# Moving the memory's preparation ahead of the second latent keys in a two-layer decoder trunk

## The chip, the cores and the metric

The kernel runs on one core of a Trainium2 chip. The time is that of the device in microseconds, from one launch, as the median of several executions. The engines are TensorE (PE, matrix products; PEld its weight loads), VectorE (DVE), ScalarE (ACT), GpSimd (POOL) and SyncE (SP). [...]

## The reference

Two layers over 512 tokens of width 1024, in float32. A layer has three attention branches that share one input `h = RMSNorm(x)`, and then an MLP:

```python
dq, dk, dv, c_q, c_kv_kr, xq, gate_logits = split(h @ w_in)
y_diff = diff_attention(dq, dk, dv) @ w_diff_o             # 8 heads, two softmax maps each
y_mla  = latent_attention(c_q, c_kv_kr) @ w_mla_o          # 8 heads, keys and values from a 256-wide latent
mem_n  = rmsnorm(mem, mem_gain)                            # 256 fixed memory tokens
y_mem  = memory_cross_attention(xq, mem_n, w_mem_kv) @ w_cross_o   # 4 heads
x = x + (sig(g0)*y_diff + sig(g1)*y_mla + sig(g2)*y_mem) @ w_out
x = x + relu(rmsnorm(x) @ w1)**2 @ w2
```

The memory is the same in both layers; its gain and its weights `w_mem_kv` are the layer's own. Its keys and values depend on nothing that the layer computes from `x`.

## The kernel before

The activations lie transposed, 512 tokens along the free dimension in tiles of 128 x 512. Every float32 operand of a large product is split into a rounded part and a remainder (`split_into`, `split_scaled`: the first on ScalarE, L103 and L107, the second on VectorE, L104 and L108), and each product is three matmuls (`mm3`, L111 to L113). Weights are loaded by SyncE into five tiles `wraw`, and split into `whi` and `wlo`, three tiles deep.

**The order of the work.** The program is a list of entries, each with a function that emits instructions and the weight pieces it takes. The list is written by hand: for each layer come the two latents and their statistics (`ck_item`, `cq_item`, `stats`, `ck_finish`, `cq_finish`), and then the phases of `PLAN` (L25). A phase is a string of groups; `gx:1` takes one entry of the group `gx`. A phase also has a list of attention units, and `merge` (L47) deals the string's entries out evenly among the units. The groups that matter here:

- `gx`: eight gate products of the latent branch (`gate_item`): 24 matmuls of 128 x 512 into one accumulator `psacc`, then VectorE (L783) and a tanh on ScalarE (L784).
- `K0`, `K1`: the keys and values of heads 0 to 3 and 4 to 7 from the latent (`kvb_item`). For each of four token blocks: one accumulator, a copy of the key half into a tile of the pool `O` (L499), a split of the value half into tiles of the pool `B` (L107, L108). Then the keys' squares, their norms, the normed keys in four `O` tiles, and four transposes (`heads_T`, L484) that ScalarE copies into four `B` tiles (L100).
- `Q0`, `Q1`: the queries of the same heads (`qb_item`), in the same manner, with four `O` tiles (L535) and four `B` tiles (L100).
- `mem`: the memory's two preparing entries, held in a list called `pre`, and its eight projection entries (`mem_chunk`).

`pre` holds `mem_stats` (layer 0 alone) and `mem_begin`. `mem_stats` reads the memory in four pieces on ScalarE's DMA queue into `B` tiles (L209), squares each into a further `B` tile with a running sum (L210), and ends with a power on POOL. `mem_begin` transfers the transposed memory in four pieces into `B` tiles (L328), and splits each with the layer's gain in two halves into a pair of `O` tiles (L107, L108); the eight `O` tiles are read by the projection.

Phase 0 has no attention units. Phase 1 has those of heads 0 to 3 of the latent attention (`mla_att`): scores (L624, L627), maximum, exponential (L641), a scaling (L100), and in every second unit transposes of the probabilities (L668), their splits, the product with the values into `pso`, and its split into `O` tiles.

**What decides when an instruction runs.** The entries give every instruction a place in the order; a scheduler with a timing model then deals them out to the engines at compile time and may let a later one go ahead of an earlier one that isn't ready. Every tile belongs to a pool with a fixed number of slots: `O` 16, `B` 40, `scr` 5, `P` 3; in PSUM `psacc` 2, `pss` 3, `pstp` 2 and `pso` 1. A tile gets its slot when it is first filled, and gives it back after its last reader.

Of the kernel before, what the change touches and what calls it, by code (L numbers as in the profile page):

```python
# [21 lines left out]
MEM = 256  # L22
EPS = 1e-6
NEG = -1.0e30
PLAN = ["gx:1 K0 gx:1 Q0 gx:1 K1 gx:1 Q1", "gx mem", "xq h0 v0", "h1 ym", "v1 h2 gc:5", "h3 v2 h4 gc:3", "h5 v3 h6 gc", "h7 gd:5", "gd"]  # L25

C_MIX, C_MLP, C_MEM, C_B, C_QA, C_KVA, C_DO, C_MQ, C_MK, C_CQ, C_CK, C_N = 0, 8, 16, 24, 48, 51, 53, 54, 55, 56, 57, 58

# [18 lines left out]
def merge(att, gemm):  # L47
    if not att:
        return gemm
    out, n, m = [], len(att), len(gemm)  # L50
    j = 0
    for i, a in enumerate(att):
        out.append(a)
        while j < m and j * n < (i + 1) * m:
            out.append(gemm[j])
            j += 1
    out.extend(gemm[j:])
    return out
# [3 lines left out]
def tile_trunk(ctx: ExitStack, tc: tile.TileContext, x_t, mem_t, mem_n, pos, ifr, gcol, grow, w_ck, w_cq, w_kvb, w_qb,  # L62
# [27 lines left out]
    def ct(name, shape, dt=F32):  # L90
        return cst.tile(shape, dt, tag=name, name=name)
# [32 lines left out]
    gc = ct("gc", [P, L, C_N])  # L124
# [79 lines left out]
    def mem_stats():  # L204
        sq4 = small("mss4", 4, 1)
        for t in range(2):
            for j in range(2):
                mt, junk = tl("B"), tl("B")
                A.dma_start(out=mt, in_=mem_n[t * P:(t + 1) * P, j * 512:(j + 1) * 512])  # L209
                A.activation(out=junk, in_=mt, func=AF.Square, accum_out=sq4[:, 2 * t + j:2 * t + j + 1])  # L210
        ss = small("mss", 2, 1)
        V.tensor_reduce(out=ss, in_=sq4.rearrange("p (t j) -> p t j", t=2), axis=AX.X, op=ALU.add)
        ms = small("msm", 2, 1)
        V.tensor_scalar(ms, ss, 1.0 / D, EPS, ALU.mult, ALU.add)
        mst["r"] = small("rmem", 2, 1)
        rsq(mst["r"], ms, 2)
        mst["eps"] = small("epsm", 2, 1)
        V.tensor_scalar(mst["eps"], ms, EPS, None, ALU.mult)
# [64 lines left out]
    def layer(l):  # L283
# [93 lines left out]
        def xq_chunk(c):  # L377
            def done(tp, q):
                if tp == 0:
                    s["xq", c] = [tl("B") for _ in range(2)]  # L380
                y = tl("scr")
                A.activation(out=y, in_=q, func=AF.Copy)
                z = tl("scr")
                A.activation(out=z, in_=y, func=AF.Square)
                ss = small("ss", 8, 4)
                V.tensor_reduce(out=ss[:, :4], in_=z.rearrange("p (g d) -> p g d", d=128), axis=AX.X, op=ALU.add)
                e = small("e", 8, 4)
                V.tensor_tensor(out=e[:, :4].rearrange("p (t h) -> p t h", t=2), in0=ss[:, :4].rearrange("p (t h) -> p t h", t=2),
                                in1=s["ex128"][:, 2 * tp:2 * tp + 2].unsqueeze(2).broadcast_to([P, 2, 2]), op=ALU.add)
                f = small("f", 8, 4)  # L390
                rsq(f[:, :4], e[:, :4], 4)
                yv = y.rearrange("p (g d) -> p g d", d=128)
                V.tensor_tensor(out=yv, in0=yv, in1=f[:, :4].unsqueeze(2).broadcast_to([P, 4, 128]), op=ALU.mult)
                tp_ = ps("tp")
                for h in range(2):
                    for t in range(2):
                        T.transpose(tp_[:, h * 256 + t * P:h * 256 + (t + 1) * P], in_=yv[:, t * 2 + h, :], identity=ident)
                for h in range(2):
                    scale_to(s["xq", c][h][:, tp * 256:(tp + 1) * 256], tp_[:, h * 256:(h + 1) * 256], col(C_CQ))
            return chunk256(w_xq[l, c], x_h, 4, done)  # L400
# [157 lines left out]
        def v_chunk(p):  # L558
            def done(tp, q):
                if tp == 0:  # L560
                    s["dv", p] = [tl("B") for _ in range(2)]
                for ti in range(2):
                    t = 2 * tp + ti
                    A.activation(out=s["dv", p][tp][:, ti * 256:(ti + 1) * 256], in_=q[:, ti * 256:(ti + 1) * 256], func=AF.Copy, scale=s["r"][:, t:t + 1])
            return chunk256(w_d[l, 8 + p], x_h, 4, done)
# [180 lines left out]
        def diff_att(h):  # L746
            p, hh = h // 2, h % 2

            def unit(qi):
                def fn(w):  # L750
                    if qi == 0:
                        s["co"], s["cs"] = ps("o"), small("osum", 8, 3)
                    N = P * (qi + 1)
                    o, cs = s["co"], s["cs"].rearrange("p (m q) -> p m q", m=2)
                    qh, ql, kk = s["dh", h]
                    v_ = s["dv", p]
                    W = max(N, 256)
                    qk = [([z[m][:, qi * P:(qi + 1) * P] for z in (qh, ql)], kk[m][:, :W]) for m in range(2)]
                    vf = lambda j: v_[j // 2][:, (j % 2) * 256 + hh * P:(j % 2) * 256 + (hh + 1) * P]
                    pt = scores(N, qk, True, [cs[:, m, qi:qi + 1] for m in range(2)], True)  # L760
                    pv_tok(pt, qi + 1, o[:, qi * P:(qi + 1) * P], vf)
                    if qi == NT - 1:
                        oc = o_copy()
                        z = tl("scr")
                        A.activation(out=z, in_=oc, func=AF.Square)
                        ss = small("ss", 8, 4)
                        V.tensor_reduce(out=ss[:, :4], in_=z.rearrange("p (g d) -> p g d", g=4), axis=AX.X, op=ALU.add)
                        e = small("e", 8, 4)
                        V.tensor_tensor(out=e[:, :4], in0=cs[:, 0, :], in1=cs[:, 0, :], op=ALU.mult)
                        V.scalar_tensor_tensor(out=e[:, :4], in0=e[:, :4], scalar=128.0 * EPS, in1=ss[:, :4], op0=ALU.mult, op1=ALU.add)  # L770
                        f = small("of", 8, 3)
                        rsq(f[:, :4], e[:, :4], 4)
                        o_finish(oc, f[:, :4], 4, dgain[:, l:l + 1], "od")
                return Entry(fn)
            return [unit(q) for q in range(NT)]

        def gate_item(b, ft, where):
            def fn(w):
                q = ps("acc")
                for k in range(KT):  # L780
                    mm3(q, (w[0][0][:, k, :], w[0][1][:, k, :]), s["h"][k], k == 0, k == KT - 1)
                g = tl(where)
                V.tensor_tensor(out=g, in0=q, in1=s["R"], op=ALU.mult)  # L783
                A.activation(out=g, in_=g, func=AF.Tanh, scale=0.5, bias=hb[:, l, b * 8 + ft:b * 8 + ft + 1])  # L784
                s["g", b, ft] = g
            return Entry(fn, [w_g[l, b * 8 + ft]])
# [10 lines left out]
        def y4_item(w_o, key, b, fp, first):  # L797
            def fn(w):
                for i in range(2):
                    q = ps("acc")  # L800
                    for k in range(4):
                        mm3(q, (w[0][0][:, i * 4 + k, :], w[0][1][:, i * 4 + k, :]), s[key][k], k == 0, k == 3)
                    y_mix(q, b, 2 * fp + i, first)
            return Entry(fn, [w_o[l, fp]])
# [154 lines left out]
        def gy4(w_o, key, b, first):  # L959
            r = []  # L960
            for fp in range(4):
                r += [gate_item(b, 2 * fp, "G"), gate_item(b, 2 * fp + 1, "G"), y4_item(w_o, key, b, fp, first)]
            return r

        e = [Entry(lambda w: begin())]
        gx = [gate_item(1, ft, "X") for ft in range(KT)]
        ym = [y4_item(w_om, "om", 1, fp, True) for fp in range(4)]
        gc_ = gy4(w_oc, "oc", 2, False)
        gd = [gate_item(0, ft, "B") for ft in range(KT)]
        cross = sum([cross_att(h) for h in range(4)], [])  # L970
        mem = sum([mem_chunk(c) for c in range(4)], [])
        e += [Entry(ck_item, [w_ck[l][:, 0:2, :], w_ck[l][:, 2:5, :], w_ck[l][:, 5:8, :]]), cq_item(0), Entry(lambda w: stats()), cq_item(1), Entry(lambda w: ck_finish()), cq_item(2), Entry(lambda w: cq_finish())]
        pre = ([Entry(lambda w: mem_stats())] if l == 0 else []) + [Entry(mem_begin)]
        K0, K1, Q0, Q1 = [kvb_item(0)], [kvb_item(1)], [qb_item(0)], [qb_item(1)]
        xq = xq_chunk(0) + xq_chunk(1)
        groups = {"gx": gx, "K0": K0, "K1": K1, "Q0": Q0, "Q1": Q1, "mem": pre + mem, "xq": xq, "ym": ym, "gc": gc_, "gd": gd}
        groups.update({f"v{p}": v_chunk(p) for p in range(4)}, **{f"h{h}": head_chunk(h) for h in range(8)})

        def take(spec):
            r = []  # L980
            for t in spec.split():
# [6 lines left out]
                  diff_att(4) + diff_att(5), diff_att(6) + diff_att(7), []]  # L988
        for a, sp in zip(phases, PLAN):
            e += merge(a, take(sp))  # L990
# [16 lines left out]
    for l in range(L):  # L1007
        prog.extend(layer(l))
# [157 lines left out]
```

## Time and profile before

| | |
|---|---|
| median of 3 runs | 1997.16 us (1996.64 to 2002.54) |
| the profiled execution: time, span | 1999.83 us, 1998.0 us |
| PE busy | 1956.1 us, 98% of the span |
| DVE, ACT, POOL busy | 68%, 52%, 15% |
| mean granted clock of TensorE | 0.997 |
| DMA | 181.20 MB, mean 91 GB/s |

A row of the order in time has the start in us, the duration, the engine, the line and operation, the tiles as out<-in, their shapes, a count, and in brackets the engine's idle time just before and what ended it. `ACTq` is ScalarE's queue of instructions as it issues a DMA. Names are given without their numbers, so that `B` stands for any tile of the pool `B`. Layer 0 ends at about the middle of the span: what happens at 77 us in layer 0 happens at 1071 us in layer 1.

### The profile page before, as it was taken

To read this page: it belongs to the slowest core of one execution; us is meant where nothing else is said; L and a number is where in the kernel's file an instruction comes from. 1 tells how busy PE (TensorE), PEld (TensorE's weight loads), DVE (VectorE), ACT (ScalarE), POOL (GpSimd) and SP (SyncE) were. 2 spreads that over 40 slices of the span, in tenths; PEclk is the share of its full clock that TensorE was granted. 3 is DMA by queue.
4 is the path that set the end of the run, shared out by engine and by line. 5 is a ranking of instruction groups with operands and counts; after the bars stand their busy time and mean duration, and the time that the engine had idled before them with its cause. 6 is when DMAs were issued, how large, how long until landed. Compare 5 with 4: busy or idle time off the path is not lost.

```text
span 1998.0 us, 30334 instructions
## 1 busy us (share of the span) xinstructions
PE 1956.1 (98%) x11888; PEld 1739.9 (87%) x11888; DVE 1352.1 (68%) x2431; ACT 1029.5 (52%) x1929; POOL 305.6 (15%) x209
## 2 busy tenths in 40 slices
PE   8999999999999999999999999999899999999999
PEld 7779989888888899999888899988888888999997
DVE  7756677687745866666657667677777458666665
ACT  5666765555533533344456667555555335344332
POOL 0300101111100222222002001011111002222220
PEclk9999999999999999999999999999999999999999
DMA  5233122222224233333432321121222332232232
GB/s 182 69 112 106 64 64 72 67 69 70 74 64 158 64 106 106 97 104 95 132 113 68 119 92 55 64 76 63 64 74 79 101 126 75 96 106 96 95 107 83
DMA packets 54687, 181.20 MB, mean 91 GB/s; under 512 B 6417, under 2 KB 7441, under 8 KB 54545
## 3 DMA queue, kind: packets, MB, share of 16 engines
q1 hardware_dynamic: 51840, 175.66, 27.2%
q10 hardware_dynamic: 2704, 3.62, 0.6%
q8 instruction: 93, 1.52, 0.3%
q14 instruction: 50, 0.40, 0.1%
HBM read 175.06 MB, written 4.19 MB: 90 GB/s over the span
## 4 chain that ended last, share of the span: by engine, by line
PE 90%; DVE 5%; ACT 2%; issue 1%; DMA 1%; ACTq 0%; DVEq 0%
PE psacc L111 20%; PE psacc L112 20%; PE psacc L113 20%; PE pss L113 5%; PE pss L111 5%; PE pss L112 5%; PE pss L627 2%; PE pso L656 2%; PE pss L624 1%; PE pstp L113 1%; PE pstp L112 1%; PE pstp L111 1%; PE pstp L668 1%; DVE wlo L104 1%; PE pstp L652 1%
## 5 line engine op out<-in xcount | busy, mean ns | idle before, releaser
L103 ACT ACTIVATE whi<-wraw 128x1024 fp32r<-128x1024 f32 (+1 forms) x362 | 378.7, 1047 | 522.6 <-PE psacc L112 225.0
L104 DVE TENSOR_TENSOR wlo<-wraw,whi 128x1024 fp32r<-128x1024 f32 (+1 forms) x362 | 444.6, 1228 | 126.1 <-ACT whi L103 124.4
L111 PE MATMUL psacc<-B,whi 128*128 128x512 f32 x1072 | 421.2, 393 | 2.7 <-DVE G L783 2.7
L112 PE MATMUL psacc<-B,whi 128*128 128x512 f32 x1072 | 419.5, 391 | 0.0
L113 PE MATMUL psacc<-B,wlo 128*128 128x512 f32 x1072 | 418.6, 390 | 0.0
L111 PE MATMUL psacc<-whi,B 128*128 128x256 f32 (+3 forms) x1008 | 302.0, 300 | 14.7 <-ACT whi L103 6.9
L112 PE MATMUL psacc<-wlo,B 128*128 128x256 f32 (+3 forms) x1008 | 295.5, 293 | 1.2 <-DVE wlo L104 1.2
L113 PE MATMUL psacc<-whi,B 128*128 128x256 f32 (+3 forms) x1008 | 293.4, 292 | 0.0
L1055 POOL TENSOR_TENSOR wraw<-wraw,wraw 128x1024 f32<-128x1024 f32 x56 | 152.7, 2726 | 572.0 <-DVE wlo L104 501.9
L111 PEld LDWEIGHTS psacc<-B,whi 128*128 128x128 f32 x1072 | 201.6, 188 | 42.9 <-DVE G L783 3.5
L113 PEld LDWEIGHTS psacc<-B,wlo 128*128 128x128 f32 x1072 | 201.4, 188 | 42.2
L112 PEld LDWEIGHTS psacc<-B,whi 128*128 128x128 f32 x1072 | 201.6, 188 | 37.8
L111 PEld LDWEIGHTS psacc<-whi,B 128*128 128x128 f32 x1008 | 192.9, 192 | 22.7 <-ACT whi L103 6.9
L112 PEld LDWEIGHTS psacc<-wlo,B 128*128 128x128 f32 x1008 | 193.1, 192 | 5.0 <-DVE wlo L104 1.5
L113 PEld LDWEIGHTS psacc<-whi,B 128*128 128x128 f32 x1008 | 192.6, 192 | 1.7
L947 DVE TENSOR_TENSOR X<-psacc,X 128x512 f32<-128x512 f32 x128 | 88.3, 690 | 135.3 <-PE psacc L113 135.3
L111 PE MATMUL pss<-O,whi 128*128 128x256 f32 (+1 forms) x528 | 170.2, 323 | 1.6 <-ACT whi L103 0.9
L112 PE MATMUL pss<-O,whi 128*128 128x256 f32 (+1 forms) x528 | 170.3, 322 | 0.0
L113 PE MATMUL pss<-O,wlo 128*128 128x256 f32 (+1 forms) x528 | 169.7, 323 | 0.3 <-DVE wlo L104 0.3
L136 POOL TENSOR_TENSOR f<-e,mhalf 128x8 f32<-128x8 f32 (+1 forms) x60 | 89.3, 1488 | 469.2 <-DVE e L583 270.3
L641 ACT ACTIVATE P<-pss,nmx 128x128 f32<-128x128 f32 (+2 forms) x224 | 115.4, 521 | 47.9 <-DVE nmx L638 35.7
L111 PEld LDWEIGHTS pss<-O,whi 128*128 128x128 f32 x528 | 100.4, 190 | 13.2 <-ACT whi L103 3.5
(250 smaller groups left out, 3563.9 us busy)
## 6 DMA issues: line engine op xcount, KB each, us to landing
wraw<-in_w_dram SPq DMA_DIRECT2D x128, 512.0 KB, 3.5
wraw<-in_w_g_dram SPq DMA_DIRECT2D x48, 512.0 KB, 3.5
wraw<-in_w_d_dram SPq DMA_DIRECT2D x48, 512.0 KB, 3.7
wraw<-in_w_mem_dram SPq DMA_DIRECT2D x16, 512.0 KB, 3.7
wraw<-in_w_od_dram SPq DMA_DIRECT2D x16, 512.0 KB, 3.6
wraw<-in_w_out_dram SPq DMA_DIRECT2D x16, 512.0 KB, 3.9
X<-in_x_t_dram SPq DMA_DIRECT2D x16, 256.0 KB, 5.1
wraw<-in_w_xq_dram SPq DMA_DIRECT2D x8, 512.0 KB, 3.7
```

The source lines that it names most:

```text
L103: A.activation(out=hi, in_=src, func=AF.Copy)
L104: V.tensor_tensor(out=lo, in0=src, in1=hi, op=ALU.subtract)
L111: T.matmul(o, lhsT=l[0], rhs=r[0], start=first, stop=False, **kw)
L112: T.matmul(o, lhsT=l[0], rhs=r[1], start=False, stop=False, **kw)
L113: T.matmul(o, lhsT=l[1], rhs=r[0], start=False, stop=last, **kw)
L136: G.tensor_tensor(out=o, in0=e, in1=mhalf[:, :n], op=ALU.pow)
L624: T.matmul(sw[m][:, :max(N, 256)], lhsT=qk[m][0][i], rhs=qk[m][1], start=i == 0, stop=i == 1)
L627: T.matmul(sv[m], lhsT=qk[m][0], rhs=qk[m][1], start=True, stop=True)
L641: A.activation(out=pt[:, m, :N], in_=sv[m], func=AF.Exp, bias=nmx[:, m:m + 1], accum_out=ssum[m])
L656: T.matmul(o, lhsT=w[:, j * P:(j + 1) * P], rhs=vs(j), start=j == 0, stop=j == nb - 1)
L947: V.tensor_tensor(out=xt, in0=q, in1=xt, op=ALU.add)
L1055: G.tensor_tensor(out=d["t"], in0=src[0]["t"], in1=src[1]["t"], op=ALU.subtract)
```

## The change

The two entries of `pre` become a group of their own. `PLAN` takes it in phase 0, behind the first queries and ahead of the third gate product and the second keys; `mem` keeps the eight projection entries in phase 1. Phase 1 then deals 12 entries out among its eight attention units, where it had 14 in layer 0 and 13 in layer 1.

```diff
-PLAN = ["gx:1 K0 gx:1 Q0 gx:1 K1 gx:1 Q1", "gx mem", "xq h0 v0", ...
+PLAN = ["gx:1 K0 gx:1 Q0 pre gx:1 K1 gx:1 Q1", "gx mem", "xq h0 v0", ...
...
         pre = ([Entry(lambda w: mem_stats())] if l == 0 else []) + [Entry(mem_begin)]
...
-        groups = {"gx": gx, "K0": K0, "K1": K1, "Q0": Q0, "Q1": Q1, "mem": pre + mem, "xq": xq, ...
+        groups = {"gx": gx, "K0": K0, "K1": K1, "Q0": Q0, "Q1": Q1, "pre": pre, "mem": mem, "xq": xq, ...
```

More of the change, by code (lines that the diff above doesn't have):

```diff
@@ L24 @@
 NEG = -1.0e30
-PLAN = ["gx:1 K0 gx:1 Q0 gx:1 K1 gx:1 Q1", "gx mem", "xq h0 v0", "h1 ym", "v1 h2 gc:5", "h3 v2 h4 gc:3", "h5 v3 h6 gc", "h7 gd:5", "gd"]
+PLAN = ["gx:1 K0 gx:1 Q0 pre gx:1 K1 gx:1 Q1", "gx mem", "xq h0 v0", "h1 ym", "v1 h2 gc:5", "h3 v2 h4 gc:3", "h5 v3 h6 gc", "h7 gd:5", "gd"]
 C_MIX, C_MLP, C_MEM, C_B, C_QA, C_KVA, C_DO, C_MQ, C_MK, C_CQ, C_CK, C_N = 0, 8, 16, 24, 48, 51, 53, 54, 55, 56, 57, 58
@@ L975, in layer @@
         xq = xq_chunk(0) + xq_chunk(1)
-        groups = {"gx": gx, "K0": K0, "K1": K1, "Q0": Q0, "Q1": Q1, "mem": pre + mem, "xq": xq, "ym": ym, "gc": gc_, "gd": gd}
+        groups = {"gx": gx, "K0": K0, "K1": K1, "Q0": Q0, "Q1": Q1, "pre": pre, "mem": mem, "xq": xq, "ym": ym, "gc": gc_, "gd": gd}
         groups.update({f"v{p}": v_chunk(p) for p in range(4)}, **{f"h{h}": head_chunk(h) for h in range(8)})
```

## The prediction

> **What bounds the kernel now.** I read the page first, then the busy time by windows around the two places that the change touches, then ScalarE's instructions in order of time, and last TensorE's beside them. From the page:
>
> ```profile
> span 1998.0 us, 30334 instructions
> PE 1956.1 (98%) x11888; PEld 1739.9 (87%) x11888; DVE 1352.1 (68%) x2431; ACT 1029.5 (52%) x1929; POOL 305.6 (15%) x209
> PE 90%; DVE 5%; ACT 2%; issue 1%; DMA 1%; ACTq 0%; DVEq 0%
> ```
>
> TensorE sets the time: 98% busy, 90% of the chain that ended last. No matrix work is added or taken away, so the change can only move TensorE's idle time (42 us in all) and its clock. The windows (columns: stretch, length, busy time by engine, granted clock, DMA share, GB/s) show what the memory's preparation costs where it stands now, first in layer 0, then in layer 1:
>
> ```profile
> 128.30:138.30 10.00, 5.39 (x22) 3.25 (x22) 6.61 (x18) 9.38 (x26) 0.70 (x1) 0.95 0.56 176
> 138.30:143.80 5.50, 5.48 (x25) 5.48 (x26) 4.72 (x11) 5.42 (x15) 0.00 (x0) 0.50 0.17 63
> 1120.00:1128.60 8.60, 7.12 (x34) 4.42 (x32) 6.23 (x14) 7.57 (x20) 0.00 (x0) 1.00 0.42 150
> ```
>
> In layer 0 TensorE idles 10.00 - 5.39 = 4.6 us, while ScalarE is busy 9.38 of 10; behind it follow 5.5 us at a granted clock of 0.50, which is 5.5 x 0.5 = 2.75 us lost. In layer 1, without the statistics, it idles 8.60 - 7.12 = 1.5 us and the clock holds. So 4.6 + 2.75 + 1.5 = 8.9 us is all that a perfect move could win, 0.45% of the time.
>
> Why it is so long in layer 0 is read on ScalarE (L209 reads the memory for its statistics, L210 squares it, L328 transfers the transposed memory, L107 splits it):
>
> ```profile
> 122.36 0.35 ACTq L209 DMA_DIRECT2D B<-in_mem_n_dram  x1
> 122.61 0.71 ACT L784 ACTIVATE X<-X,hb 128x512 f32<-128x512 f32 x1
> 123.22 0.67 ACT L100 ACTIVATE B<-pstp,gc 96x512 f32<-96x512 f32 x1
> 125.04 0.63 ACT L210 ACTIVATE B<-B 128x512 f32<-128x512 f32 x1 [1.14 <-DMA B<-in_mem_n_dram]
> 125.04 0.35 ACTq L209 DMA_DIRECT2D B<-in_mem_n_dram  x1
> ...
> 128.65 0.63 ACT L210 ACTIVATE B<-B 128x512 f32<-128x512 f32 x1 [2.89 <-DMA B<-in_mem_n_dram]
> 128.66 0.33 ACTq L209 DMA_DIRECT2D B<-in_mem_n_dram  x1
> ...
> 131.21 0.34 ACTq L209 DMA_DIRECT2D B<-in_mem_n_dram  x1
> ...
> 134.21 0.65 ACT L210 ACTIVATE B<-B 128x512 f32<-128x512 f32 x1
> 134.42 0.33 ACTq L328 DMA_DIRECT2D B<-in_mem_t_dram  x1
> ...
> 137.76 0.91 ACT L107 ACTIVATE O<-B,gc 128x256 fp32r<-128x256 f32 x2 [0.27 <-DMA B<-in_mem_t_dram]
> ...
> 142.22 0.90 ACT L107 ACTIVATE O<-B,gc 128x256 fp32r<-128x256 f32 x2
> DMA to landing us min/median/max: 2.5/2.6/3.6
> DMA to landing us min/median/max: 3.0/3.8/6.7
> ```
>
> (The last two rows are the landings of the reads for the statistics and of the transfers.) The four reads go out one by one, each together with the square of the one before. The chain from the first read to the first transfer takes 134.42 - 122.36 = 12.1 us, and from there to the end of the last split 143.12 - 134.42 = 8.7 us.
>
> **How tiles are granted.** The reads could have gone out at any time since the start: they depend on nothing. They go out right behind the last copy of a query into a tile of the pool B (L100), and the read that fills a B tile follows the square that fills the B tile named before it. I read this so: the tiles of one pool are granted strictly in the order in which the program names them, each when the first instruction that fills it is placed. The second keys show the same (L499 copies the keys into O, L107 splits the values into B, L100 copies the turned queries into B):
>
> ```profile
> 51.79 0.37 ACT L499 ACTIVATE O<-psacc 128x256 f32<-128x256 f32 x1
> 52.05 0.47 ACT L107 ACTIVATE B<-psacc,skv 128x256 fp32r<-128x256 f32 x1
> ...
> 77.55 0.39 ACT L499 ACTIVATE O<-psacc 128x256 f32<-128x256 f32 x1
> ...
> 82.59 0.68 ACT L100 ACTIVATE B<-pstp,gc 96x512 f32<-96x512 f32 x1 [0.81 <-PE pstp L484]
> 83.17 0.82 ACT L107 ACTIVATE B<-psacc,skv 128x256 fp32r<-128x256 f32 x2
> ...
> 1071.02 0.39 ACT L499 ACTIVATE O<-psacc 128x256 f32<-128x256 f32 x1 [0.36 <-PE psacc L113]
> ...
> 1076.05 0.68 ACT L100 ACTIVATE B<-pstp,gc 96x512 f32<-96x512 f32 x1 [0.81 <-PE pstp L484]
> 1076.64 0.82 ACT L107 ACTIVATE B<-psacc,skv 128x256 fp32r<-128x256 f32 x2
> ```
>
> In the first keys the split follows its copy by 0.3 us. In the second keys it comes 5.6 us after it, in both layers, right behind the fourth query copy, though the product is ready and B has six of its 40 tiles free (16 for the normed input, 4 and 6 for the two latents, 4 values and 4 keys are 34). Only the order explains that. TensorE pays at once, since both accumulators then hold unread keys:
>
> ```profile
> 84.45 0.50 PE L111 MATMUL psacc<-whi,B 128*128 128x512 f32 x1 [1.24 <-DVE B L108]
> 85.94 0.81 PE L627 MATMUL pss<-B,B 96*128 96x384 f32 x2
> 87.97 1.88 PE L627 MATMUL pss<-B,B 96*128 96x512 f32 x4
> 1077.91 0.50 PE L111 MATMUL psacc<-whi,B 128*128 128x512 f32 x1 [1.24 <-DVE B L108]
> ```
>
> **The change part by part.** The instructions are the same; what moves is the place in the order, and with it the place in three queues: ScalarE's, the grant of B and the grant of O.
>
> *What it takes away.* The gaps at 128 to 138 and 1120 to 1128 lose their cause: ScalarE has 4 squares and 8 splits less there. I leave 0.4 and 0.5 us for the attention's own waits: 4.2 and 1.0 us won. The slow clock after the first gap goes too, 2.75 us.
>
> *What it puts behind the second keys, layer 0.* Their values come after the memory's 4 x 2 tiles for the statistics and 4 raw tiles in B, and their key copies after the memory's 8 split tiles in O. So nothing reads the two accumulators until the whole preparation is placed, its last split included. It starts where the fourth query copy is, 82.6. B then has 38 tiles taken, so one read and its square fit at a time. By the measured chain it takes 12.1 us. With the quickest landing and nothing else in the way it takes 4 x 2.5 = 10; with the slowest landing, each read also waiting for the square before it (0.63), 4 x 4.2 = 17. I take 12.5, near the measured chain. The transfers and splits took 8.7 us between the attention's work; by themselves they take the first landing, 137.76 - 134.42 = 3.3, and 8 x 0.45 = 3.6, together 6.9. Two transfers at a time would take 2 x (3.8 + 1.9) = 11.4. I take 7.3, since by then four attention tiles have come free. Then copy, split and remainder until the matmul, 84.45 - 83.17 = 1.3 and the copy's 0.3: 82.6 + 12.5 + 7.3 + 1.6 = 104.0 against 84.45, 19.5 us later (bounds: 10 + 6.9 for the two, 16.6 later; 17 + 11.4, 28.1 later). TensorE fills this only with scores that it does between 84 and 90 now, 0.81 + 1.88 = 2.7 at most, 2.4 taken. The gate products stand behind the keys in the accumulators, and the attention's transposes behind the key and query transposes in the pool of turned tiles. That leaves 17.1 us of idle. The clock will be at 0.50 behind it as it is behind the gap now: 2.75 us, which cancels the 2.75 won. Layer 0: 17.1 - 4.2 = +12.9.
>
> *Layer 1.* Only the four transfers and eight splits, from 1076.1. Two transfers at a time end after 11.4 us, four at once after 3.8 + 3.6 = 7.4. The matmul at 1077.91 moves to 1089.1 or 1085.1, that is 11.2 or 7.2 us; I take 9.0 (with the quickest landing, 3.0, it is 6.4). Less 2.4 of scores and 1.0 won: +5.6. The clock may fall here too: half of 2.75, 1.4. Layer 1: +7.0.
>
> *The rest.* The order of the weight loads on SyncE's queue and of the gate and memory products is kept; the attention's places between them shift by one product at most, which I cost at nothing because both are TensorE work. POOL's one power of the statistics waits earlier, with only powers behind it that the second keys and queries need, and these are later anyway. The memory's 8 split tiles hold half of O (16) while the second queries are built; keys and queries need 2 + 4 + 4, the last of which follow the release of the first, so again nothing, up to 5 us if not.
>
> Sum: +12.9 + 7.0 = +19.9. The profiled execution took 1999.83 us (span 1998.0), 2.7 above the median of 1997.16; I add to the median: 2017.
>
> On the clock the row is 5.5 us at 0.50 after gaps of which none is longer than 1.7 us. [...]
>
> **Rivals.** *The reads simply go earlier, and are hidden (faster).* If tiles are granted to whoever is ready, the preparation spreads over ScalarE's idle time from 60 us on, the second keys are not held, and only the gains stay: -4.2 - 2.75 - 1.0, 1989. For it: ScalarE is busy 52%, and DMA engines have room. Against it: the split 5.6 us behind its copy in both layers. It decides if the key copy still follows its product at once. [...] The trace shows no early issue here: the reads have no input and still went out at 122.
>
> *Only B holds, O does not.* Key copies run at once, and the values wait for the last transfer's issue, not for the splits. Layer 0: 82.6 + 12.5 + 1.8 + 1.3 = 98.2, 13.7 later, less 2.4 and 4.2: +7.1. Layer 1: 0 to 5 us later, less 2.4 and 1.0: -3 to +2. Time 2001 to 2006. For O's order I have one weak sign, a split that waited on ScalarE until a tile named before it was filled:
>
> ```profile
> 1115.83 0.33 ACTq L328 DMA_DIRECT2D B<-in_mem_t_dram  x1
> ...
> 1120.97 0.69 ACT L641 ACTIVATE P<-pss,nmx 128x512 f32<-128x512 f32 x1 [3.62 <-PE pstp L668]
> ...
> 1127.12 0.38 ACT L103 ACTIVATE O<-pso 64x256 fp32r<-64x256 f32 x1
> ...
> 1128.05 0.90 ACT L107 ACTIVATE O<-B,gc 128x256 fp32r<-128x256 f32 x2
> ```
>
> With the median landing the first transfer was in by about 1119.6, and ScalarE idled 3.6 us until 1120.97; the first split into O came at 1128.05, behind the attention's first copy into O.
>
> *The move changes nothing*, because placing goes by readiness and the reads stay at 122: 1997.
>
> **How the numbers follow.** Held keys, both pools: 0.76, with its own range 2009 (16.6 - 2.7 - 4.6 and 6.4 - 2.7 - 1.5, +11.5) to 2030 (28.1 - 2.1 - 4.2 and 11.2 - 2.1 - 0.5 + 2.75, +33; 2.1 is the least of scores). B alone: 0.10, most of it above +0.3%. Hidden reads: 0.10. No move: 0.04. A measurement of this kernel tells about 0.3%, 6 us, from no change. Faster 0.10; same 0.04 and 0.04 of B alone, 0.08; slower 0.82. The range goes down to 1998, to take in B alone, and up to 2030.
>
> **What would show it.** Right: the first read directly behind the fourth copy of the first queries near 82; no key copy of the second keys between about 78 and 100 in layer 0; TensorE idle there some 15 us and at 0.50 behind it; the gaps at 128 to 138 (shifted) gone; in layer 1 a gap of some 7 us without reads. Wrong: key copies at 77 to 80 as now, reads before the fourth copy, or a chain of reads well away from 12 us.

## The result, and the profile after

The changed kernel takes 2018.25 us (median of 5 runs, 2017.27 to 2019.78) against 1997.69 (5 runs, 1996.64 to 2002.95): a ratio of 1.0097 [1.0082, 1.0112]. It is slower by 1%; 2017 was predicted. The profiled execution took 2017.27 us, 17.4 above that of before.

From the page of the changed kernel:

```profile
span 2015.5 us, 30352 instructions
PE 1960.4 (97%) x11888; PEld 1743.2 (86%) x11888; DVE 1352.7 (67%) x2431; ACT 1031.7 (51%) x1929; POOL 309.7 (15%) x209
```

TensorE idles 2015.5 - 1960.4 = 55.1 us where it idled 41.9: 13.2 us more. Its busy time grew by 4.3 us with the same 11888 matmuls, while its mean granted clock fell from 0.997 to 0.990. The two together are the 17.5 us of the span.

Where it happened is read from two lines of SyncE's queue: L956, which writes the stream out as the last products of layer 0 end, and L951, which writes the output. Each row has, for one line, the count, the duration of the issue in ns (least, median, most), and the start of the first and of the last in us. First the kernel before:

```profile
L956 SPq DMA_DIRECT2D xs_dram<-X x8: 319/320/331, 987.9 to 1008.9; - x8
L951 SPq DMA_DIRECT2D out_dram<-X x8: 332/332/344, 1976.1 to 1995.1; - x8
```

and the changed one:

```profile
L956 SPq DMA_DIRECT2D xs_dram<-X x8: 319/320/330, 997.6 to 1018.6; - x8
L951 SPq DMA_DIRECT2D out_dram<-X x8: 332/332/344, 1993.5 to 2012.5; - x8
```

Layer 0 became 997.6 - 987.9 = 9.7 us longer, and the stretch from there to the first output 995.9 - 988.2 = 7.7.

ScalarE in order of time, layer 0, from the first queries' fourth copy on:

```profile
81.69 0.68 ACT L100 ACTIVATE B<-pstp,gc 96x512 f32<-96x512 f32 x1 [1.06 <-PE pstp L484]
81.70 0.35 ACTq L209 DMA_DIRECT2D B<-in_mem_n_dram  x1
84.64 0.63 ACT L210 ACTIVATE B<-B 128x512 f32<-128x512 f32 x1 [0.63 <-DMA B<-in_mem_n_dram]
85.39 0.35 ACTq L209 DMA_DIRECT2D B<-in_mem_n_dram  x1
...
88.43 0.33 ACTq L209 DMA_DIRECT2D B<-in_mem_n_dram  x1
...
91.02 0.33 ACTq L209 DMA_DIRECT2D B<-in_mem_n_dram  x1
...
93.65 0.82 ACTq L328 DMA_DIRECT2D B<-in_mem_t_dram  x2
...
97.63 2.66 ACT L107 ACTIVATE O<-B,gc 128x256 fp32r<-128x256 f32 x6 [0.24 <-DMA B<-in_mem_t_dram]
100.20 0.36 ACT L499 ACTIVATE O<-psacc 128x256 f32<-128x256 f32 x1
100.47 0.46 ACT L107 ACTIVATE B<-psacc,skv 128x256 fp32r<-128x256 f32 x1
```

The first read goes out with the fourth query copy, as forecast. (A row of `ACTq` is the issue of a transfer, and can stand ahead of the copy that it follows: here and in the kernel before, where the read at 122.36 stands ahead of the fourth copy at 123.22, it goes out within 0.05 us of the end of the transposes that this copy waits for, 81.65 and 122.32.) No key copy of the second keys (L499) stands between it and the last memory split: the copy that was at 77.55 is now at 100.20, and its value split follows it by 0.3 us where it followed by 5.6. TensorE, in layer 0 and in layer 1:

```profile
101.50 0.79 PE L111 MATMUL psacc<-whi,B 128*128 128x512 f32 x1 [10.54 <-DVE B L108]
...
1098.13 0.80 PE L111 MATMUL psacc<-whi,B 128*128 128x512 f32 x1 [3.22 <-DVE B L108]
```

and the busy times by windows (stretch, length, busy time by engine, granted clock, DMA share, GB/s):

```profile
81.50:101.50 20.00, 6.37 (x17) 2.99 (x15) 10.60 (x29) 13.40 (x40) 0.69 (x1) 0.58 0.34 105
101.50:105.10 3.60, 3.60 (x9) 2.83 (x10) 1.59 (x5) 1.22 (x4) 1.64 (x1) 0.50 0.00 0
143.10:152.00 8.90, 8.90 (x72) 8.55 (x71) 4.48 (x7) 8.21 (x19) 0.00 (x0) 1.00 0.18 62
1085.50:1098.10 12.60, 6.67 (x15) 2.90 (x13) 9.41 (x26) 10.61 (x32) 0.00 (x0) 0.61 0.25 83
1098.10:1101.80 3.70, 3.67 (x9) 2.90 (x10) 1.78 (x5) 1.19 (x3) 1.64 (x1) 0.50 0.00 0
```

TensorE idles 20.00 - 6.37 = 13.6 us of the first stretch and 5.9 of the fourth. Behind each it works some 3.6 us at a clock of 0.50; the last section shows when the clock fell. The third row is the place where the preparation stood: TensorE is busy all through it, so the old gap is gone.

### The profile page after: what moved, and what is told of

Read it like the earlier page. It is cut to its first block, busy times and chain, and to the rows that moved or that the text cites. A ratio compares the mean times of both kernels' runs of the same rounds, so it can differ in the third digit from the quotient of the medians.

```text
span 2015.5 us, 30352 instructions
## 1 busy us (share of the span) xinstructions
PE 1960.4 (97%) x11888; PEld 1743.2 (86%) x11888; DVE 1352.7 (67%) x2431; ACT 1031.7 (51%) x1929; POOL 309.7 (15%) x209
## 4 chain that ended last, share of the span: by engine, by line
PE 91%; DVE 5%; ACT 1%; issue 1%; DMA 1%; ACTq 0%; DVEq 0%
PE psacc L111 20%; PE psacc L112 20%; PE psacc L113 20%; PE pss L113 5%; PE pss L111 5%; PE pss L112 5%; PE pss L627 2%; PE pss L624 2%; PE pso L656 2%; PE pstp L113 1%; PE pstp L112 1%; PE pstp L111 1%; PE pstp L668 1%; DVE wlo L104 1%; PE pstp L652 1%
## 5 line engine op out<-in xcount | busy, mean ns | idle before, releaser
L136 POOL TENSOR_TENSOR f<-e,mhalf 128x8 f32<-128x8 f32 (+1 forms) x60 | 93.5, 1558 | 470.2 <-DVE e L583 260.5
L111 PEld LDWEIGHTS pss<-O,whi 128*128 128x128 f32 x528 | 100.4, 190 | 13.2 <-ACT whi L103 3.5
```

The costliest lines, as they stand in the source:

```text
L111: T.matmul(o, lhsT=l[0], rhs=r[0], start=first, stop=False, **kw)
L136: G.tensor_tensor(out=o, in0=e, in1=mhalf[:, :n], op=ALU.pow)
```

## The experiments

The theory is that of the prediction: tiles are granted pool by pool in the order of the program, so that the second keys' values (B) and key copies (O) wait for the memory's whole preparation. Its rivals are that ScalarE's own order holds them, and that B alone does. The edits are against the changed kernel. The first four ran on one chip beside 23 runs of the kernel before (median 1999.6, from 1994.67 to 2003.5), the last four on another beside 20 (2000.01, 1995.2 to 2003.84).

### The statistics alone moved

```diff
-        "pre": pre, "mem": mem
+        "pre": pre[:-1], "mem": pre[-1:] + mem
```

> Only the four reads, squares and the power of the statistics move to between the first queries and the second keys; the transfers and splits stay where they were before the change. Theory A (tiles of a pool are granted in the order of the program, in B and in O): the O tiles of the second keys are no longer behind anything, so their key copies follow their products at about 77 us as before the change; the value splits (B) still come after the fourth square, near 93 us, and the third product of the second keys starts at about 95 us (84.5 before, 101.5 with the whole change). Layer 1 is as before. Layer 0: 10.5 us later, less 2 of scores, 1.8 for the clock, and some 6 us won at the old gap: about +4, 2002 us (1999 to 2005). Theory B (ScalarE takes the preparation first because it stands earlier, whatever pool it fills): the key copies come after the fourth square too, behind 93 us, with about the same time.

Measured: 2004.85 us (10 runs), ratio 1.003 [1.0019, 1.004]. ScalarE, in order of time:

```profile
78.34 0.39 ACT L499 ACTIVATE O<-psacc 128x256 f32<-128x256 f32 x1
79.95 0.38 ACT L499 ACTIVATE O<-psacc 128x256 f32<-128x256 f32 x1 [1.22 <-PE psacc L113]
...
95.06 0.63 ACT L210 ACTIVATE B<-B 128x512 f32<-128x512 f32 x1 [1.94 <-DMA B<-in_mem_n_dram]
...
95.69 0.82 ACT L107 ACTIVATE B<-psacc,skv 128x256 fp32r<-128x256 f32 x2
```

The statistics fill only B tiles. The key copies into O go on as before, and the value splits into B, which read the same accumulators on the same engine, come 15.7 us later (95.69 against 79.95, the second copy), directly behind the last square. If ScalarE took the preparation first whatever it fills, the key copies would have waited too; so it is the pool. The third product came at 96.81 us (95 expected). In layer 1, which has no statistics, this kernel is 1.3 us longer than before (989.5 against 988.2); what makes it so was not shown.

### The transfers and splits alone moved

```diff
-        "pre": pre, "mem": mem
+        "pre": pre[-1:], "mem": pre[:-1] + mem
```

> Only the transfers and splits move; the statistics stay ahead of the projection. Theory A: layer 1 is as with the whole change (third product 10 us later, +7.8 us). Layer 0 does the same from 81.7 us: two transfers at a time, key copies only after the last split, third product at about 94.5; the chain of reads remains in the attention but without transfers and splits behind it, so some 2 to 4 us of the old loss go: about +7 in layer 0, +15 in all, 2013 us (2009 to 2016). If O were granted out of order the key copies would stand at 77 us, the third product at about 88 to 91, and the time would be about 2003.

Measured: 2007.39 us (8 runs), ratio 1.0038 [1.0025, 1.0051]: below the range given. ScalarE:

```profile
82.78 0.83 ACTq L328 DMA_DIRECT2D B<-in_mem_t_dram  x2
...
89.80 0.34 ACTq L328 DMA_DIRECT2D B<-in_mem_t_dram  x1
...
92.63 0.90 ACT L107 ACTIVATE O<-B,gc 128x256 fp32r<-128x256 f32 x2
93.43 0.37 ACT L499 ACTIVATE O<-psacc 128x256 f32<-128x256 f32 x1
```

Now the key copies are held as well. B asks the values to wait for the last transfer's issue, at 89.80; the key copy into O waits on until the last split into O, at 92.63. So O is granted in order too, and the rival with B alone falls. The third product came at 95.22, 94.5 expected.

The miss is in what is won. In layer 0 this kernel is only 2.3 us longer than before (its L956 row begins at 990.2), in layer 1 7.7, as the full change is. The reads for the statistics still stand in phase 1, 10 us later with all that is around them, and yet the old gap is gone. The reads' line, and the window over it:

```profile
L209 ACTq DMA_DIRECT2D B<-in_mem_n_dram x4: 334/334/335, 132.7 to 141.3; - x4
```

```profile
130.00:160.00 30.00, 30.00 (x209) 27.37 (x208) 17.30 (x32) 21.68 (x49) 2.72 (x3) 1.00 0.45 150
```

TensorE is busy in all 30 us while the four reads run. ScalarE is hardly earlier there. Its first split of the attention's turned probabilities comes 6.9 us behind the issue of the first read in the kernel before, and TensorE idles until then:

```profile
129.28 0.58 ACT L103 ACTIVATE PT<-pstp 128x512 fp32r<-128x512 f32 x1
129.91 0.49 PE L111 MATMUL pso<-PT,B 128*128 128x512 f32 x1 [1.65 <-ACT PT L103]
```

In the kernel with the splits alone it comes 6.6 us behind the issue, and TensorE has memory products from 138.40 on and doesn't wait:

```profile
139.38 0.58 ACT L103 ACTIVATE PT<-pstp 128x512 fp32r<-128x512 f32 x1
140.86 0.40 PE L111 MATMUL pso<-PT,B 128*128 128x512 f32 x1
```

So the reads and squares don't make the gap alone. It opens where ScalarE is late and TensorE has no memory products ready; with the splits done early it has them.

### One tile for a read and its square

```diff
-                mt, junk = tl("B"), tl("B")
+                mt = tl("B")
...
-                A.activation(out=junk, in_=mt, func=AF.Square, ...
+                A.activation(out=mt, in_=mt, func=AF.Square, ...
```

> The whole change, with each square written over the tile that was read, so that the statistics fill four B tiles in place of eight. Theory A: a read no longer stands behind the square before it in the order of B, only behind a free tile (two are free): reads one and two go out together near 82 us, three and four near 86; the first transfer goes out near 88.5 in place of 93.65, and the third product of the second keys starts near 97 in place of 101.5: about 4.5 us less than with the change, 2013.5 us. Rival (reads go out singly because ScalarE's queue holds them): reads stay 3 us apart, no change, 2018 us.

Measured: 2015.73 us (4 runs, 2011.85 to 2017.34), ratio 1.0074 [1.005, 1.0098].

```profile
82.86 0.83 ACTq L209 DMA_DIRECT2D B<-in_mem_n_dram  x2
...
89.69 0.44 ACTq L328 DMA_DIRECT2D B<-in_mem_t_dram  x1
```

Two reads go out together, the other two follow at 86.28 and 89.32, and the chain from the first read to the first transfer takes 6.8 us, not 11.95. So the chain's length came from the tiles, not from the reads. Of these 5.1 us, only 2.8 came out at the third product (98.67, not 101.50, where 97 was expected): the chain began 1.2 us later, and from the first transfer on it took 1.1 us longer. The time is above the 2013.5 expected, and its interval overlaps that of the full change, so the gain in time alone is not settled; the rows are.

### The preparation's tiles from another pool, place kept

```diff
-                mt, junk = tl("B"), tl("B")
+                mt, junk = tl("PT"), tl("PT")
...
-                raw = tl("B")
+                raw = tl("PT")
```

> The whole change, with the tiles of the statistics and the raw transfers taken from the pool PT (4 tiles, unused until the attention), not from B. Theory A: reads and transfers no longer stand behind the query copies and go out long before 60 us; the second keys' value splits are not held, their key copies only until the last split of the memory (O), which has its data long before: first key copy by about 80 us; the gap at 122 to 138 us is gone in layer 0 and that of layer 1 too. Time 1989 to 1993 us, faster than before the change; reads right at the start could cost up to 5 us there, since the DMA engines are full from 8 to 16 us. Theory B (ScalarE's order alone): reads stay at 82 us and the time at 2018.

Measured: 1994.45 us (10 runs, 1991.58 to 1996.27), ratio 0.9971 [0.9961, 0.9981]. The place in the program is that of the slow kernel; only the pool differs, and the kernel is now faster than before. The two lines that load, the first with its landings:

```profile
L209 ACTq DMA_DIRECT2D PT<-in_mem_n_dram x4: 335/346/352, 5.7 to 23.9; - x4
DMA to landing us min/median/max: 4.6/5.6/7.0
...
L328 ACTq DMA_DIRECT2D PT<-in_mem_t_dram x8: 334/344/446, 28.6 to 577.0; - x8
```

PT isn't used until the attention, so nothing named earlier holds it, and the reads go out at 5.7 us. For layer 1 the transfers are out by 577.0, in the middle of layer 0. The second keys' copies are back at 78.47, and the third product's wait is the old 1.2 us. The time is 1.5 us above the range expected (1989 to 1993). Some is paid at the start: the first matmul of the layer's own statistics (L240) runs at 20.87 us against 20.19 before, and the ninth at 51.17 against 49.77.

The four reads still go out one by one, over 18 us, though PT's four tiles hold two reads with their squares. A read waits until the tile of the square before it, named ahead of it, is being filled, and that waits for the landing. So the serial chain has two causes, each enough by itself: the order of the names, which the version with one tile per read takes away, and the number of free tiles, which by the rows held its third and fourth read (issued at 86.28 and 89.32, behind the first and second square).

### The preparation behind the second keys

```diff
-PLAN = ["... Q0 pre gx:1 K1 gx:1 Q1", ...
+PLAN = ["... Q0 gx:1 K1 pre gx:1 Q1", ...
```

> The whole preparation one place later: behind the second keys, ahead of the fourth gate product and the second queries. Theory A: the second keys run as before the change (key copies at 77 and 79 us, third product at about 84.5); now the second queries are held: the first read goes out behind the fourth copy of the second keys (102.9 before the change, some 2 us earlier with TensorE free), some 18.6 us later the last split ends, the queries' copies into O follow, and the third product of the second queries starts near 119 in place of 98. With nothing but key transposes to fill it: layer 0 about +14, layer 1 (transfers alone, 11 us) about +10, 2022 us (2015 to 2030). Rival (the hold belongs to the second keys, for instance because nothing else could be placed): near the time before the change, 1990 to 2000.

Measured: 2027.87 us (4 runs, 2024.77 to 2028.3), ratio 1.0144 [1.0126, 1.0163]. The second keys run as before, with the third product at 84.99. The second queries are held instead, by their copies into O (L535):

```profile
124.67 0.69 PE L111 MATMUL psacc<-whi,B 128*128 128x384 f32 x1 [23.44 <-ACT O L535]
```

This third product of the second queries was expected at 119; the time is in the range given. The wait is TensorE's longest in all the kernels here. The wait belongs to whatever the program names next in the same pool, not to the keys.

### The preparation behind the second queries, three ways

The place alone, with the tiles in B; with the tiles from PT; and with the tiles from `scr`, the square written over its input:

```diff
-PLAN = ["... Q0 pre gx:1 K1 gx:1 Q1", ...
+PLAN = ["... Q0 gx:1 K1 gx:1 Q1 pre", ...
```

> The whole preparation behind the second queries, at the end of phase 0. Theory A: in the order of B it stands where it stood before the change, so the reads go out at the same place, behind the fourth copy of the second queries (122 us); nothing of phase 0 is held. In O it now stands ahead of the attention's first output tiles, so the splits come a little earlier and the attention's first output waits for them. The gap at 128 to 138 stays: 1998 us (1993 to 2003). Rival (an earlier place in the list moves the reads): reads before 110 us, about 1991.

> As the one with the tiles of the pool PT, but placed behind the second queries: reads and transfers again go out from the start of the kernel, the splits into O come behind the second queries' O tiles (105 us), where ScalarE has gaps of 3 to 4 us. Theory A: second keys as before the change (values split behind the fourth query copy near 83 us), no gap at 128 to 138. With the start slowed as in the run with PT (about 2 us): 1992 us (1989 to 1995), 1 to 3 us below that run.

> The whole preparation behind the second queries, with its tiles for reads and transfers taken from the pool scr (5 tiles) and the squares written over what was read. Theory A: in the order of scr it stands behind the squares of the second queries, whose last is at 105.7 us, so the reads go out near 106 and not at the start, four or five together; transfers near 113, splits done by about 120 while TensorE has gate products; nothing is held, the start is not slowed, and no gap is left at 128 to 138. Layer 0 about -7, layer 1 about -1: 1990 us against 1998 before (1988 to 1994).

Measured: place alone 1997.11 us (10 runs), ratio 0.9991 [0.9982, 1.0001]; with PT 1993.65 (10 runs), 0.997 [0.9959, 0.9981]; with `scr` 1989.01 (5 runs, 1988.41 to 1990.23), 0.9956 [0.994, 0.9972].

The first has the same 12 entries in phase 1 as the full change, so it also shows that dealing out 12 in place of 14 costs nothing that can be told. Its reads go out at 122.72, behind the query copies as before, and the old gap stays. The version with `scr` is faster than both kernels:

```profile
104.14 0.83 ACTq L209 DMA_DIRECT2D scr<-in_mem_n_dram  x2
105.02 0.93 ACTq L209 DMA_DIRECT2D scr<-in_mem_n_dram  x2
...
108.11 0.92 ACTq L328 DMA_DIRECT2D scr<-in_mem_t_dram  x2
...
114.41 2.51 ACT L107 ACTIVATE O<-scr,gc 128x256 fp32r<-128x256 f32 x6 [0.69 <-DMA scr<-in_mem_t_dram]
```

All four reads are out within 2 us, between the second queries' copies and without waiting for the B tiles of those queries. The waits of TensorE from 48 to 200 us (total, count, longest) are then only the two that the kernel before also has:

```profile
PE psacc L111 <- DVE B L108: 2.4, 2, 1.2
PE pstp L484 <- ACT B L100: 0.8, 1, 0.8
```

Layer 0 ends at 980.9 us, 7.0 earlier than before, and layer 1 is 4.3 shorter. Between medians the version wins 11.0 us, more than the 8.9 that the prediction called all that a perfect move could win; the next section shows where. What makes this version faster than the one with PT wasn't separated: place of the reads, pool and the single tile differ together.

## Why the prediction was right

**The mechanism** was held by each of its own marks: first read at 81.70 (82.6 foreseen), no key copy between 78 and 100, a clock of 0.50 behind the gap (it had fallen ahead of it, as the last section shows), the old gap gone, a shorter gap in layer 1. The reading that carried it was the row of before in which a value split stood 5.6 us behind its copy with tiles free. The experiments show each half of it: B in the kernel with the statistics alone, O in the one with the splits alone. For O the prediction had one weak sign; it is now shown. That the pool and not the place is the cause is shown by the same place with another pool, 1994 in place of 2018.

**The sizes.** The same TensorE instruction in two traces tells how much later it runs (start in us; the last column is for the version with `scr`):

| instruction | before | changed | later by | `scr` |
|---|---|---|---|---|
| start: first L240 | 20.19 | 19.46 | -0.73 | -0.75 |
| layer 0, ahead of the old gap's place: transposes of the second queries, L484 | 121.28 | 137.42 | 16.14 | -0.06 |
| behind it: L599 | 379.39 | 386.70 | 7.31 | -9.47 |
| later: L599 | 530.11 | 539.86 | 9.75 | -7.01 |
| layer 1, ahead of the old gap's place: L484 | 1114.75 | 1133.89 | 19.15 | -7.06 |
| behind it: L599 | 1367.15 | 1383.18 | 16.03 | -10.14 |
| later: L599 | 1518.37 | 1535.80 | 17.43 | -11.36 |

*Layer 0*: +12.9 predicted, +9.7 measured. The hold cost 16.9 us; the prediction's terms for it are 19.5 - 2.4 + 2.75 = 19.85. All its parts were taken too long: the fourth copy came 0.9 earlier (0.7 of it from the start), the read chain took 93.65 - 81.70 = 11.95 (12.5 taken), transfers and splits 100.29 - 93.65 = 6.6 (7.3), the way from there to the matmul 1.2 (1.6). The third product came 17.05 later, and the scores done in the wait then took off more than the clock's 3.6 x 0.5 = 1.8 added: 0.9 less, where 2.75 - 2.4 = 0.35 more was taken. The old place gave back 8.8, where 4.2 + 2.75 = 6.95 was taken. With `scr` it is about as much, so idle time and clock as the rows of before show them understate what the gap cost; why is open. And 2.4 us came between 379 and 530 us, where nothing was forecast. The version with `scr` loses as much there, so this isn't the hold.

*Layer 1*: +7.0 predicted, +7.7 measured. The hold cost 9.4 (9.0 - 2.4 + 1.4 = 8.0 taken). The third product moved from 1077.91 + 9.7 = 1087.6 to 1098.13, 10.5 us (9.0 taken, between 7.2 for four transfers at a time and 11.2 for two). ScalarE shows why it is near the upper end:

```profile
1085.61 0.82 ACTq L328 DMA_DIRECT2D B<-in_mem_t_dram  x2
...
1089.86 0.33 ACTq L328 DMA_DIRECT2D B<-in_mem_t_dram  x1
...
1092.38 0.33 ACTq L328 DMA_DIRECT2D B<-in_mem_t_dram  x1
```

Two go out, and the others one by one as the raw tiles come free: no attention tile helped. The old place gave back 3.1 (1.0 taken), again more than its idle time of 1.5. The two old places so cost 8.8 + 3.1 = 11.9 us and not 8.9. The last 1.4 us come around 1460, where the changed kernel's clock is at 0.50 for 3.42 us (1460.41 to 1463.83) and that of the kernel before stays at 1.00; whether the change brought this was not shown.

**The sum** was 19.9 and is 17.4 between the profiled executions and 20.6 between the medians; the profiled execution of before lies 2.1 above its median of five runs, that of after 1.0 below, and runs of the kernel before spread from 1994.67 to 2003.84. Errors of 1 to 3 us with both signs cancel in it, and it lacks 3.8 us that came at other places. That 2017 lies so near 2018.25 is luck; that the kernel slows by about 1%, and why, is not.

**The rivals.** The hidden reads fall with the reads at 81.70. Once the tiles come from a pool in which nothing else waits, what that rival foresaw comes about: it gave 8.0 us under the kernel before, and 5.2 (PT) and 11.0 (`scr`) were measured. As ratios these are -0.29% and -0.44%, against +1.0% with the tiles in the pool B.

What the prediction had wrong in its picture of the old gap: it put the gap down to ScalarE's load of squares and splits. The kernel with the splits alone showed that ScalarE being late there costs TensorE nothing once memory products are ready. And its reason for the serial reads, two free tiles, was only one of two.

## What to carry to other kernels

Moving independent work earlier in a program doesn't start it early, as here, if its tiles are granted in program order from a pool in which tiles named earlier are still to be filled; it only puts everything named later in that pool behind it. Before such a move, find in the trace an instruction that runs late though its inputs are ready and tiles are free, and see what was named ahead of it. Give the moved work a pool of its own, or one that is idle at that point, and place it where the critical engine has work that is already fed.

## What the runs showed of the hardware

The granted clock of TensorE is 1.00 from 20 to 1997 us but for these stretches (columns as above), first in the kernel before:

```profile
137.26:144.09 6.83, 5.77 (x27) 5.77 (x28) 5.61 (x13) 6.32 (x17) 0.00 (x0) 0.50 0.29 87
454.70:458.11 3.41, 3.41 (x18) 3.41 (x17) 0.76 (x2) 0.00 (x0) 0.00 (x0) 0.50 0.00 0
```

and then in the changed kernel:

```profile
84.84:105.32 20.48, 8.60 (x18) 5.33 (x18) 10.04 (x27) 13.04 (x37) 2.33 (x2) 0.50 0.29 90
463.72:467.13 3.41, 3.41 (x18) 3.41 (x17) 0.30 (x2) 0.00 (x0) 0.00 (x0) 0.50 0.00 0
1088.36:1102.01 13.65, 9.44 (x19) 5.39 (x18) 9.08 (x25) 10.35 (x29) 1.64 (x1) 0.50 0.12 39
1460.41:1463.83 3.42, 3.42 (x19) 3.42 (x18) 0.15 (x1) 0.25 (x1) 0.00 (x0) 0.50 0.02 5
```

In the changed kernel the clock so fell at 84.84 and at 1088.36, among the scores, where the longest wait of TensorE in the 10 us before was 1.75 us, and not in the waits of 10.54 and 3.22 that came later. In the kernel before it fell at 137.26, 0.6 us into a wait of 1.67.

It came back at 144.09 in the kernel before, and at 105.32 and 1102.01 in the changed one: 5.8, 3.8 and 3.9 us after TensorE's last wait ended (138.32, 101.50, 1098.13). The 4.63 us of scores from 86.32 on, without a wait, ran at 0.50 and left the clock there. What sets these times was not shown; the prediction took the 5.5 us of before for the changed kernel too.

The four reads for the statistics took 4.6 to 7.0 us to land with the tiles from PT, issued at 5.7 to 23.9 us (row above). The same four reads of the changed kernel, issued at 81.7 to 91.0 us, have this row:

```profile
DMA to landing us min/median/max: 2.5/2.6/2.9
```
